# Element-wise work of the mLSTM heads moved from GpSimd to VectorE in a one-layer hybrid trunk

## The chip, the core and the metric

The kernel runs on one core of a Trainium2 chip. The metric is the device time of one launch in microseconds (us); lower is better. The engines named below are PE (TensorE, matmuls), DVE (VectorE), ACT (ScalarE), POOL (GpSimd) and SP (SyncE, which issues every DMA of this kernel). In the code they are `T`, `V`, `A`, `G` and `nc.sync`.

## What is computed

One layer of a hybrid decoder on a prompt of 1024 tokens and on 32 sample tokens (8 sequences of 4). Shapes: width 1024, four mLSTM heads of 128, 512 S5 channels.

```python
proj = rmsnorm(h) @ w_in                       # x_m, z_m, o_m, gates, x_s, z_s
xc = silu(conv4(x_m));  q, k, v = per head of xc, xc, x_m
# chunkwise mLSTM, per head and chunk, m_t the running max:
s   = (q k^T) * exp(b_t - b_s + i_s - m_t)     # causal
num = s v + decay * (q C);  qn = s.sum + decay * (q n)
hA  = num / max(|qn|, exp(-m_t));  C, n = dl * (C, n) + sum wl k (v, 1)
hA  = (layernorm(hA * sigmoid(o)) * ln_head + skip * xc) * silu(z_m)
yB  = gelu(s5_scan(x_s));  yB = yB * sigmoid(yB @ w_glu + b) * silu(z_s)
h   = h + concat(hA, yB) @ w_out
h   = h + sigmoid(h @ w_ple_gate) * rmsnorm(p @ w_ple);  y = rmsnorm(h)
```

The outputs are y and the new states (C, n, m, convolution, S5) of the prompt and of the samples. All of it is fp32.

## The kernel before

Large products are made as three passes, since each fp32 operand is split into a rounded `hi` part and a rest `lo = x - hi` (`mm3`, L123 to L125: hi*hi, hi*lo, lo*hi). In time the program goes through the projections of x_s and o (to about 100 us), the S5 scan (to 240), the mLSTM heads (240 to 400), the rest of the gated unit of S5, called glu here (to about 430), w_out (431 to 540) and w_ple_gate (540 to the end).

The order of PE is written by hand (`tc.manual_schedule`): `turns` runs the generators of two prompt heads (0 and 1, then 2 and 3) in turn, a piece of a sample head between them, and after each piece `take(n)` puts n columns of other matmuls (projections of x_m, z_m, z_s, then the glu) as fill. The order of the other engines, SP too, is made by a scheduler from a simulated timeline, so an instruction that changes its engine shifts others. Each engine works strictly in its order.

What the change touches, for one head and one half of 512 tokens (`mlstm`):

- L1132 loads `nmb` (a row of decay exponents, broadcast by DMA from DRAM); L1133 adds the causal mask `cmask`. L1154 (ACT) takes its exponential and L1155 (DVE) multiplies it with the scores `sps` in PSUM.
- L1137 makes `qps`, L1138 (ACT) copies it to `qp`; L1163 makes `qd = qp * dcb`, which the matmul L1171 reads. L1145 makes `xw` from the transposed `xc`.
- L1175 to L1180 update state and output; `lnorm` (L1206 to L1226) normalises, with a power on POOL at L56; its last four instructions L1226 write what PE transposes at L1188 (`tph`).
- The tail of a half: ACT `sk` L1190, DVE L1191, then L1194 multiplies `sk` with the gate `zt` and a DMA writes it to DRAM.

For the samples (`sample_head`), four times per head: L1298 spreads v over sequence pairs under a mask (`svm`, 96x258), the matmul L1300 makes `sups`, two instructions L1302 add it to the state. L1326 and L1328 (`sample_end`) apply skip and gate of the 32 tokens. `wload` loads the weights of w_out and w_ple_gate; its rest L1353 (`wol`, `wgl`) is made by POOL for odd k and by DVE for even k. In the glu, L1034 makes the rest `yl` of its input, which L124 of `mm3` multiplies; L1482 makes the rest `mlo` of the heads' output.

PSUM pools: `pv` has two buffers (vps, qps, tpxc, sps), `pg` one (all of the sample head), `pt` one (tph).

Of the kernel before, what the change touches and what calls it, by code (L numbers as in the profile page):

```python
# [8 lines left out]
F32 = mybir.dt.float32  # L9
# [3 lines left out]
MUL, ADD, SUB, MAX, MIN = ALU.mult, ALU.add, ALU.subtract, ALU.max, ALU.min  # L13
# [16 lines left out]
def tile_hymba(ctx: ExitStack, tc: tile.TileContext, d: dict, o: list):  # L30
    nc = tc.nc
    (y_p, y_s, o_pC, o_pn, o_pm, o_pconv, o_pre, o_pim, o_sC, o_sn, o_sm, o_sconv, o_sre, o_sim) = o
    V, A, G, T = nc.vector, nc.scalar, nc.gpsimd, nc.tensor
# [307 lines left out]
    skp = hcols[:, 4:8]  # L341
# [85 lines left out]
    k = 1  # L427
# [14 lines left out]
    for tr_, ti_, l0, n in ((rAr, rAi, 3, 3), (rBr, rBi, 6, 4)):  # L442
        for s in range(n):
            k = 1 << s
# [91 lines left out]
    zt = s5p.tile([128, 512], F32, name="zt")  # L536
# [198 lines left out]
    cmask = mlc.tile([128, 128], F32, name="cmask")  # L735
# [341 lines left out]
    mt8 = mo.tile([128, 8, 32], F32, name="mt8")  # L1077
    xcs = mlc.tile([128, 4, 32], F32, name="xcs")
# [42 lines left out]
    def mlstm(h, v1, xc):  # L1121

        Cst = None
        tail = None
        for t in range(2):
            sl = slice(512 * t, 512 * t + 512)
            gc = 8 * h + 4 * t

            nmb = mo.tile([128, 4, 128], F32, tag="nmb", name="nmb", bufs=2)
            dcb = mo.tile([128, 4, 128], F32, tag="dcb", name="dcb", bufs=2)  # L1130
            for t_, x in ((nmb, 0), (dcb, 1)):
                dma(t_, d_row[x, h, 4 * t:4 * t + 4].unsqueeze(0).to_broadcast([128, 4, 128]))  # L1132
            G.tensor_tensor(nmb, nmb, cmask.unsqueeze(1).to_broadcast([128, 4, 128]), op=ADD)  # L1133

            qp = mo.tile([128, 512], F32, tag="qp", name="qp", bufs=2)
            ps = pv([128, 512], "qps")
            T.matmul(ps, Gm[:, h, :], xc[:, sl], start=True, stop=True)  # L1137
            A.copy(qp, ps)  # L1138
            yield
            xw = mo.tile([128, 4, 128], F32, tag="xw", name="xw", bufs=2)  # L1140
            tp = pv([128, 4, 128], "tpxc")
            for c in range(4):
                cc = 4 * t + c
                T.transpose(tp[:, c, :], xc[:, 128 * cc:128 * cc + 128], ident)
            V.tensor_tensor(xw, tp, colv[:, 1, gc:gc + 4].unsqueeze(2).to_broadcast([128, 4, 128]), op=MUL)  # L1145
            yield
            sp = pv([128, 4, 128], "sps")
            for c in range(4):
                cc = 4 * t + c
                T.matmul(sp[:, c, :], xc[:, 128 * cc:128 * cc + 128], qp[:, 128 * c:128 * c + 128],  # L1150
                         start=True, stop=True)
            sd = nmb
            for c in range(4):
                A.activation(sd[:, c, :], nmb[:, c, :], AF.Exp, bias=colv[:, 0, gc + c:gc + c + 1])  # L1154
            V.tensor_tensor(sd, sd, sp, op=MUL)  # L1155
            so4 = mo.tile([128, 4, 128], F32, tag="so4", name="so4", bufs=2)
            dma(so4, d_so[4 * t:4 * t + 4, :, 128 * h:128 * h + 128].rearrange("c p v -> p c v"))
            yield
            if tail is not None:
                tail()  # L1160
                yield
            qd = ml.tile([128, 4, 128], F32, tag="qd", name="qd", bufs=2)
            G.tensor_tensor(qd, qp.rearrange("p (c x) -> p c x", x=128), dcb, op=MUL)  # L1163

            hs = qd
            qn = ml.tile([128, 4], F32, tag="qn", name="qn", bufs=2)
            for c in range(4):
                nu = pn([128, 2, 129], "nu")
                T.matmul(nu[:, 0, :], sd[:, c, :], v1[:, 4 * t + c, :], start=True, stop=Cst is None)
                if Cst is not None:  # L1170
                    T.matmul(nu[:, 0, :], qd[:, c, :], Cst, start=False, stop=True)  # L1171
                T.matmul(nu[:, 1, :], xw[:, c, :], v1[:, 4 * t + c, :], start=True, stop=True)
                Cn = ml.tile([128, 129], F32, tag="Cst", name="Cst", bufs=4)
                if Cst is None:
                    V.tensor_copy(Cn, nu[:, 1, :])  # L1175
                else:
                    V.scalar_tensor_tensor(Cn, Cst, dcb[:, c, 127:128], nu[:, 1, :], op0=MUL, op1=ADD)
                Cst = Cn
                V.tensor_copy(qn[:, c:c + 1], nu[:, 0, 128:129])
                V.scalar_tensor_tensor(hs[:, c, :], so4[:, c, :], 1.0, nu[:, 0, 0:128], op0=ADD, op1=MUL)  # L1180
                if c == 3:
                    lnorm(hs, qn, colv[:, 2, gc:gc + 4], 128, 4)
                yield

            def tail(t=t, sl=sl, hs=hs):
                tp = pt([128, 4, 128], "tph")
                for c in range(4):
                    T.transpose(tp[:, c, :], hs[:, c, :], ident)  # L1188
                sk = ml.tile([128, 512], F32, tag="sk", name="sk", bufs=2)
                A.mul(sk, xc[:, sl], skp[:, h:h + 1])  # L1190
                V.scalar_tensor_tensor(sk, tp.rearrange("p c x -> p (c x)"), lnh[:, h:h + 1], sk, op0=MUL, op1=ADD)  # L1191
                zt = mo.tile([128, 512], F32, tag="zt", name="zt", bufs=2)
                dma(zt, d_z[h, :, sl])
                G.tensor_tensor(sk, sk, zt, op=MUL)  # L1194
                dma(d_m0[t][h], sk)


        fps = pn([128, 129], "fps")
        T.matmul(fps, wk[:, h, :], Cst, start=True, stop=True)
        fo = ml.tile([128, 129], F32, tag="Cst", name="fo", bufs=4)  # L1200
        A.mul(fo, fps, SC)
        dma(o_pC[0, 0, h], fo[:, 0:128])
        V.tensor_copy(pnc[:, h:h + 1], fo[:, 128:129])
        yield
        tail()
        yield  # L1206

# [28 lines left out]
    def sample_head(h):  # L1236
# [13 lines left out]
        for i in range(3):  # L1250
# [7 lines left out]
        v3 = ml.tile([96, 129], F32R, tag="sv3", name="sv3")  # L1258
# [5 lines left out]
                               op0=MUL, op1=SUB)  # L1264
# [30 lines left out]
        for b0, nb in ((0, 2), (2, 2), (4, 2), (6, 2)):  # L1295
            ups = pg([128, 2, 129], "sups")
            vm = ml.tile([96, 2, 129], F32R, tag="svm", name="svm", bufs=1)
            G.tensor_tensor(vm[:, :nb], v3.bitcast(F32).unsqueeze(1).to_broadcast([96, nb, 129]),  # L1298
                            bmask[:, b0:b0 + nb].unsqueeze(2).to_broadcast([96, nb, 129]), op=MUL)
            T.matmul(ups[:, :nb, :], kw3, vm[:, :nb], start=True, stop=True)  # L1300
            for b in range(nb):
                V.scalar_tensor_tensor(c0[:, b0 + b, :], c0[:, b0 + b, :], dl[:, b0 + b], ups[:, b, :],  # L1302
                                       op0=MUL, op1=ADD)
            if b0 < 6:
                yield
# [4 lines left out]
    def sample_end():  # L1310
        tp = pg([32, 128], "tpn")
        T.transpose(tp, snc.rearrange("p b h -> p (b h)"), ident)
        ob = ml.tile([32, 128], F32, tag="skw", name="sob", bufs=1)
        A.copy(ob, tp)
        dma(o_sn[0].rearrange("b h k -> (b h) k"), ob)

        hs = shs[:, :, 0:128]
        V.scalar_tensor_tensor(hs[:, 0, :], sos, 1.0, hs[:, 0, :], op0=ADD, op1=MUL)
        lnorm(hs, shs[:, 0, 128:129], senm, 128, 1)
        tp = pg([128, 4, 32], "tpsh")  # L1320
        T.transpose(tp.rearrange("p h t -> p (h t)"), hs[:, 0, :], ident)
        zt = ml.tile([128, 4, 32], F32, tag="sxv", name="szt")
        dma(zt, d_z[0:4, :, 1024:1056].rearrange("h p t -> p h t"))
        sk = ml.tile([128, 4, 32], F32, tag="sqm", name="ssk")
        for h in range(4):
            G.tensor_scalar(sk[:, h, :], xcs[:, h, :], skp[:, h:h + 1], None, op0=MUL)  # L1326
            V.scalar_tensor_tensor(sk[:, h, :], tp[:, h, :], lnh[:, h:h + 1], sk[:, h, :], op0=MUL, op1=ADD)
        G.tensor_tensor(mt8[:, 0:4, :], sk, zt, op=MUL)  # L1328

    def prompt_end():  # L1330
        tp = pt([4, 128], "tpn")
# [12 lines left out]
    def wload(src, k, q, nm, use=None):  # L1344
        raw = pW.tile([128, 512], F32, tag="Wraw", name="Wraw", bufs=4)
        dma(raw, src[128 * k:128 * k + 128, 512 * q:512 * q + 512])
        pool = pW1 if q else pW
        hi = pool.tile([128, 512], F32R, tag="Whi", name=f"{nm}h{k}", bufs=8)
        lo = pool.tile([128, 512], F32R, tag="Wlo", name=f"{nm}l{k}", bufs=8)
        A.copy(hi, raw)  # L1350
        if use is not None:
            use(raw, k, q)
        (G if k % 2 else V).tensor_tensor(lo, raw, hi.bitcast(F32), op=SUB)  # L1353
        return hi, lo

    KO = (4, 5, 6, 7, 0, 1, 2, 3)
# [175 lines left out]
    for q in range(2):  # L1532
        for k in range(2):
            raw = pW.tile([128, 512], F32, tag="Wraw", name="Wraw", bufs=4)
# [140 lines left out]
```

## Time and profile before

| | |
|---|---|
| median of 3 runs | 663.01 us (662.4 to 669.05) |
| the profiled execution's own time | 664.25 us |
| span of the profiled execution | 662.5 us |
| mean granted TensorE clock | 0.982 of 2.4 GHz |
| PE busy | 615.7 us (93%) |
| DVE busy | 451.9 us (68%) |
| ACT busy | 254.8 us (38%) |
| POOL busy | 134.3 us (20%) |

Busy time says how long an engine had an instruction under way, whether it moved data or stood. Shares are over the whole span; stages differ, so the rows further down go stage by stage.

### The profile page before, as it was taken

To read this page: it belongs to the slowest core of one execution; us is meant where nothing else is said; L and a number is where in the kernel's file an instruction comes from. 1 tells how busy PE (TensorE), PEld (TensorE's weight loads), DVE (VectorE), ACT (ScalarE), POOL (GpSimd) and SP (SyncE) were. 2 spreads that over 40 slices of the span, in tenths; PEclk is the share of its full clock that TensorE was granted. 3 is DMA by queue.
4 is the path that set the end of the run, shared out by engine and by line. 5 is a ranking of instruction groups with operands and counts; after the bars stand their busy time and mean duration, and the time that the engine had idled before them with its cause. 6 is when DMAs were issued, how large, how long until landed. Compare 5 with 4: busy or idle time off the path is not lost.

```text
span 662.5 us, 11620 instructions
## 1 busy us (share of the span) xinstructions
PE 615.7 (93%) x4072; PEld 539.0 (81%) x4072; DVE 451.9 (68%) x1345; ACT 254.8 (38%) x622; POOL 134.3 (20%) x149
## 2 busy tenths in 40 slices
PE   5999999999999998987989897799999999999995
PEld 3999998999989986776978796677888776788885
DVE  6788969999998945996757689955222325566435
ACT  5653733333343555342331335444112225533332
POOL 6830200000000003142323523533001113010000
PEclk9999999999999997997999998899999999999999
DMA  8813345356544348362633555576341264412111
GB/s 261 240 57 57 98 145 137 90 150 152 145 109 122 99 104 237 116 209 65 171 114 118 175 165 164 187 241 213 111 152 67 92 235 141 146 49 109 63 64 64
DMA packets 112418, 90.03 MB, mean 136 GB/s; under 512 B 34080, under 2 KB 94900, under 8 KB 112360
## 3 DMA queue, kind: packets, MB, share of 16 engines
q1 hardware_dynamic: 112360, 89.29, 45.4%
q8 instruction: 32, 0.52, 0.3%
q14 instruction: 26, 0.21, 0.1%
HBM read 61.68 MB, written 27.58 MB: 135 GB/s over the span
## 4 chain that ended last, share of the span: by engine, by line
PE 60%; DVE 12%; issue 12%; DMA 11%; ACT 2%; SPq 2%; POOL 1%; POOLq 0%; DVEq 0%; ACTq 0%
PE po L1494 5%; PE po L1495 5%; PE po L1496 4%; PE po L1603 3%; PE po L1604 3%; PE po L1605 3%; PE ps_xs L123 2%; PE ps_o L123 2%; PE ps_xs L124 2%; PE ps_xs L125 2%; PE ps_o L124 2%; PE ps_o L125 2%; DMA xt<-in_x_prompt 2%; SPq L36 2%; PE ps_zs L123 2%
## 5 line engine op out<-in xcount | busy, mean ns | idle before, releaser
L1603 PE MATMUL po<-wgh,hTh 128*128 128x512 f32 (+1 forms) x136 | 52.1, 383 | 0.7 <-ACT g_t L1606 0.7
L1605 PE MATMUL po<-wgh,hTl 128*128 128x512 f32 (+1 forms) x136 | 51.5, 379 | 0.0
L1604 PE MATMUL po<-wgl,hTh 128*128 128x512 f32 (+1 forms) x136 | 51.4, 378 | 0.0
L123 PE MATMUL ps_o<-hi_o,aTh 128*128 128x264 f32 (+2 forms) x136 | 41.0, 301 | 0.0
L123 PE MATMUL ps_zs<-aTh,hi_zs 128*128 128x256 f32 (+2 forms) x96 | 39.9, 416 | 0.0
L125 PE MATMUL ps_o<-hi_o,aTl 128*128 128x264 f32 (+2 forms) x136 | 39.4, 290 | 0.0
L124 PE MATMUL ps_o<-lo_o,aTh 128*128 128x264 f32 (+2 forms) x136 | 39.4, 290 | 0.0
L123 PE MATMUL ps_xm<-aTh,hi_xm 128*128 128x256 f32 (+2 forms) x96 | 35.2, 367 | 0.0
L123 PE MATMUL ps_zm<-aTh,hi_zm 128*128 128x256 f32 (+2 forms) x96 | 32.1, 334 | 1.3 <-ACT zc L721 1.3
L1494 PE MATMUL po<-woh,mh 128*128 128x512 f32 x80 | 32.7, 409 | 0.0
L1495 PE MATMUL po<-wol,mh 128*128 128x512 f32 x80 | 32.0, 400 | 0.0
L123 PE MATMUL ps_xs<-aTh,hi_xs 128*128 128x256 f32 (+2 forms) x96 | 31.3, 326 | 0.4 <-ACT xs L287 0.4
L125 PE MATMUL ps_zs<-aTh,lo_zs 128*128 128x256 f32 (+2 forms) x96 | 31.6, 329 | 0.0
L124 PE MATMUL ps_zs<-aTl,hi_zs 128*128 128x256 f32 (+2 forms) x96 | 31.6, 329 | 0.0
L1496 PE MATMUL po<-woh,mlo 128*128 128x512 f32 x80 | 31.5, 394 | 0.0
L1503 DVE TENSOR_TENSOR hTl<-tr,hTh 128x512 fp32r<-128x512 f32 x16 | 11.0, 690 | 29.8 <-ACT hTh L1502 29.8
L125 PE MATMUL ps_xm<-aTh,lo_xm 128*128 128x256 f32 (+2 forms) x96 | 31.4, 327 | 0.0
L124 PE MATMUL ps_xm<-aTl,hi_xm 128*128 128x256 f32 (+2 forms) x96 | 31.4, 327 | 0.0
L125 PE MATMUL ps_xs<-aTh,lo_xs 128*128 128x256 f32 (+2 forms) x96 | 31.3, 326 | 0.0
L124 PE MATMUL ps_xs<-aTl,hi_xs 128*128 128x256 f32 (+2 forms) x96 | 31.3, 326 | 0.0
L125 PE MATMUL ps_zm<-aTh,lo_zm 128*128 128x256 f32 (+2 forms) x96 | 31.0, 323 | 0.0
L124 PE MATMUL ps_zm<-aTl,hi_zm 128*128 128x256 f32 (+2 forms) x96 | 31.0, 323 | 0.0
(594 smaller groups left out, 1916.4 us busy)
## 6 DMA issues: line engine op xcount, KB each, us to landing
xt<-in_x_prompt SPq DMA_DIRECT2D x15, 512.0 KB
Wraw<-in_w_out SPq DMA_DIRECT2D x16, 256.0 KB
Wraw<-in_w_ple_gate SPq DMA_DIRECT2D x16, 256.0 KB
d_h<-xt SPq DMA_DIRECT2D x8, 512.0 KB
h_t<-d_h SPq DMA_DIRECT2D x8, 512.0 KB
out<-g_t SPq DMA_DIRECT2D x14, 256.0 KB
mt<-d_m SPq DMA_DIRECT2D x10, 256.0 KB
d_us<-xs SPq DMA_DIRECT2D x32, 72.0 KB
```

The source lines that it names most:

```text
L36: nc.sync.dma_start(out, in_)
L123: T.matmul(ps, wh, xh, start=first, stop=False)
L124: T.matmul(ps, wh, xl, start=False, stop=False)
L125: last_mm[0] = T.matmul(ps, wl, xh, start=False, stop=last).ins
L1494: T.matmul(ps, mh[:, k % 4, :], hi, start=k == 4, stop=False)
L1495: T.matmul(ps, mh[:, k % 4, :], lo, start=False, stop=False)
L1496: T.matmul(ps, mlo[:, k % 4, :], hi, start=False, stop=k == 3)
L1503: V.tensor_tensor(hTl[i][:, 4 * q:4 * q + 4, :], tp, hi.bitcast(F32), op=SUB)
L1603: T.matmul(ps[:, :b - a], hTh[i][:, k, :], hi[:, ws], start=k == 4, stop=False)
L1604: T.matmul(ps[:, :b - a], hTh[i][:, k, :], lo[:, ws], start=False, stop=False)
L1605: T.matmul(ps[:, :b - a], hTl[i][:, k, :], hi[:, ws], start=False, stop=k == 3)
```

## The change

Every element-wise instruction that the heads, the sample heads and `wload` gave to POOL is given to DVE, with the same operands: per head and half L1133, L1163 and L1194 (8 of each), L1298 (16), L1326 (4), L1328 (1), and the 16 of L1353 with odd k. POOL keeps the powers (L56 and others), L1482 and some work of earlier stages. Nothing else is edited.

```diff
-            G.tensor_tensor(nmb, nmb, cmask.unsqueeze(1).to_broadcast([128, 4, 128]), op=ADD)
+            V.tensor_tensor(nmb, nmb, cmask.unsqueeze(1).to_broadcast([128, 4, 128]), op=ADD)
...
-            G.tensor_tensor(qd, qp.rearrange("p (c x) -> p c x", x=128), dcb, op=MUL)
+            V.tensor_tensor(qd, qp.rearrange("p (c x) -> p c x", x=128), dcb, op=MUL)
...
-                G.tensor_tensor(sk, sk, zt, op=MUL)
+                V.tensor_tensor(sk, sk, zt, op=MUL)
...
-            G.tensor_tensor(vm[:, :nb], v3.bitcast(F32).unsqueeze(1).to_broadcast([96, nb, 129]),
+            V.tensor_tensor(vm[:, :nb], v3.bitcast(F32).unsqueeze(1).to_broadcast([96, nb, 129]),
...
-            G.tensor_scalar(sk[:, h, :], xcs[:, h, :], skp[:, h:h + 1], None, op0=MUL)
+            V.tensor_scalar(sk[:, h, :], xcs[:, h, :], skp[:, h:h + 1], None, op0=MUL)
...
-        G.tensor_tensor(mt8[:, 0:4, :], sk, zt, op=MUL)
+        V.tensor_tensor(mt8[:, 0:4, :], sk, zt, op=MUL)
...
-        (G if k % 2 else V).tensor_tensor(lo, raw, hi.bitcast(F32), op=SUB)
+        V.tensor_tensor(lo, raw, hi.bitcast(F32), op=SUB)
```

The scheduler puts the moved instructions among those of DVE. Three places follow; a row that begins with + stands there in the changed kernel, with - in the one before, without a sign in both.

DVE, heads 0 and 1, second half (about 282 to 286 us before): the first `nmb` in the queue.

```order
 L1212 TENSOR_TENSOR ln_3881<-ln_3881,colv 128x4
-L1177 SCALAR_TENSOR_TENSOR Cst<-Cst,dcb,nu 128x129
-L1179 COPY qn<-nu 128x1
-L1219 BN_AGGR bmv<-bst 128x2
+L1133 TENSOR_TENSOR nmb<-nmb,cmask 128x512
+L1219 BN_AGGR bmv<-bst 128x2
+L1213 RECIPROCAL ln_3881<-ln_3881 128x4
+L1090 SCALAR_TENSOR_TENSOR xc<-xm,hcols,xc 128x1024
+L1177 SCALAR_TENSOR_TENSOR Cst<-Cst,dcb,nu 128x129
+L1179 COPY qn<-nu 128x1
 L1180 SCALAR_TENSOR_TENSOR qd<-so_3728,nu 128x128
```

The addition L1133, and behind it a convolution step L1090 of the next head, now stand ahead of the state update L1177.

DVE, heads 0 and 1, end of the first half's `lnorm` (about 299 to 303 us before).

```order
 L1191 SCALAR_TENSOR_TENSOR sk<-tph,hcols,sk 128x512
+L1163 TENSOR_TENSOR qd<-qp,dcb 128x512
+L1298 TENSOR_TENSOR svm<-sv_4091,bmask 96x258
 L1224 SCALAR_TENSOR_TENSOR ln_3924<-bmv,ln_3922 128x4
+L1194 TENSOR_TENSOR sk<-sk,zt 128x512
 L1226 TENSOR_SCALAR qd<-qd,ln_3922,ln_3924 128x128 x4
 L1191 SCALAR_TENSOR_TENSOR sk<-tph,hcols,sk 128x512
+L1163 TENSOR_TENSOR qd<-qp,dcb 128x512
+L1194 TENSOR_TENSOR sk<-sk,zt 128x512
 L1270 TENSOR_TENSOR ssd<-smb,ssps 32x32
```

Three instructions come to stand ahead of the four L1226 of head 1, and two behind them.

DVE, glu (about 407 to 411 us before).

```order
+L1034 SCALAR_TENSOR_TENSOR yl<-yb,yh 128x256 x2
+L1224 SCALAR_TENSOR_TENSOR ln_5253<-bmv,ln_5251 128x4
+L1226 TENSOR_SCALAR qd<-qd,ln_5212,ln_5214 128x128 x4
 L1050 SCALAR_TENSOR_TENSOR tg<-tg,yb 128x256
 L1050 SCALAR_TENSOR_TENSOR tg<-tg,ysb 128x32
-L1034 SCALAR_TENSOR_TENSOR yl<-yb,yh 128x256
-L1213 RECIPROCAL ln_5682<-ln_5682 128x1
-L1034 SCALAR_TENSOR_TENSOR yl<-yb,yh 128x256
 L1052 TENSOR_TENSOR zg<-tg,zg 128x256
```

The first two `yl` now stand ahead of the four L1226 of head 2, where before they stood behind them.

## Rows read from the trace of the kernel before

**Rows 1.** Part 1 of the page: busy us, share, instructions by engine.

```profile
PE 615.7 (93%) x4072; PEld 539.0 (81%) x4072; DVE 451.9 (68%) x1345; ACT 254.8 (38%) x622; POOL 134.3 (20%) x149
```

**Rows 2.** Windows: us, PE, PEld, DVE, ACT, POOL busy, granted clock, DMA share, GB/s.

```profile
240.00:260.00 20.00, 15.48 (x82) 12.56 (x82) 6.18 (x25) 9.83 (x25) 4.07 (x4) 0.84 0.81 211
260.00:280.00 20.00, 18.49 (x139) 16.38 (x139) 19.21 (x59) 8.50 (x18) 2.59 (x3) 0.99 0.33 101
280.00:300.00 20.00, 15.80 (x100) 13.26 (x99) 18.76 (x64) 7.94 (x21) 8.57 (x8) 1.00 0.64 198
400.00:420.00 20.00, 15.07 (x98) 13.70 (x98) 19.72 (x53) 11.50 (x25) 11.59 (x8) 0.91 0.51 155
440.00:460.00 20.00, 20.00 (x146) 15.47 (x145) 11.47 (x15) 10.66 (x18) 6.98 (x5) 1.00 0.76 238
304.00:308.00 4.00, 4.00 (x16) 3.84 (x16) 1.26 (x6) 0.77 (x2) 1.48 (x2) 0.50 0.43 140
424.00:428.00 4.00, 4.00 (x30) 3.56 (x28) 3.56 (x10) 1.96 (x3) 1.38 (x1) 0.57 0.40 136
```

**Rows 3.** Timeline of PE: start, duration, instruction, idle before and its releaser.

```profile
254.11 2.07 PE L1137 MATMUL qps<-xc,Gm 128*128 128x512 f32 x2 [2.97 <-ACT v L1105]
...
279.81 0.36 PE L1300 MATMUL sups<-svm,skw 96*128 96x258 f32 x1 [1.41 <-DVE sc L1302]
...
301.73 1.15 PE L1188 MATMUL tph<-ident,qd 128*128 128x128 f32 x4 [4.14 <-DVE qd L1226]
...
370.31 0.94 PE L1150 MATMUL sps<-qp,xc 128*128 128x128 f32 x6 [1.75 <-DVE xw L1145]
...
408.96 0.38 PE L124 MATMUL ps_g<-yl,hi_g 128*128 128x256 f32 x1 [1.94 <-DVE yl L1034]
...
421.89 0.38 PE L124 MATMUL ps_g<-yl,hi_g 128*128 128x256 f32 x1 [2.74 <-DVE yl L1034]
```

**Rows 4.** Groups of POOL: busy us, mean ns, idle before.

```profile
L1194 POOL TENSOR_TENSOR sk<-sk,zt 128x512 f32<-128x512 f32 x8 | 11.9, 1494 | 7.8 <-DVE ln L1221 7.7
L1133 POOL TENSOR_TENSOR nmb<-nmb,cmask 128x512 f32<-128x512 f32 x8 | 11.3, 1407 | 66.6 <-DMA nmb<-d_row 64.2 <-DVE sv L1260 1.9 <-DVE sv L1259 0.6
L1353 POOL TENSOR_TENSOR wol<-Wraw,woh 128x512 fp32r<-128x512 f32 x8 | 11.0, 1369 | 24.5 <-ACT woh L1350 24.4
...
L1298 POOL TENSOR_TENSOR svm<-sv,bmask 96x258 fp32r<-96x258 f32 x16 | 10.3, 645 | 63.5 <-PE sups L1300 42.0 <-DVE sv L1265 16.0 <-DMA raw_g<-in_w_glu 5.6
L1163 POOL TENSOR_TENSOR qd<-qp,dcb 128x512 f32<-128x512 f32 x8 | 10.2, 1275 | 13.5 <-DMA d_z<-ztmp 5.8 <-ACT qp L1138 3.3 <-PE tph L1188 2.8
```

**Rows 5.** Groups of DVE: busy us, mean ns, idle before.

```profile
L1052 DVE TENSOR_TENSOR zg<-tg,zg 128x256 f32<-128x256 f32 x16 | 9.8, 622 | 0.0
L1302 DVE SCALAR_TENSOR_TENSOR sc<-sc,sdc,sups 128x129 f32<-128x129 f32 x32 | 9.7, 339 | 0.6 <-PE sups L1300 0.5
L1353 DVE TENSOR_TENSOR wol<-Wraw,woh 128x512 fp32r<-128x512 f32 x8 | 7.5, 933 | 4.6 <-ACT woh L1350 4.6
L1034 DVE SCALAR_TENSOR_TENSOR yl<-yb,yh 128x256 fp32r<-128x256 f32 x16 | 7.4, 480 | 5.6 <-ACT yh L1033 5.5
```

**Rows 6.** Timeline of DVE: single instructions, start and duration.

```profile
295.54 1.10 DVE L1226 TENSOR_SCALAR qd<-qd,ln,ln 128x128 f32<-128x128 f32 x4
...
300.26 2.08 DVE L1226 TENSOR_SCALAR qd<-qd,ln,ln 128x128 f32<-128x128 f32 x4
...
398.93 0.69 DVE L1353 TENSOR_TENSOR wol<-Wraw,woh 128x512 fp32r<-128x512 f32 x1 [0.48 <-ACT woh L1350]
...
420.36 1.81 DVE L1034 SCALAR_TENSOR_TENSOR yl<-yb,yh 128x256 fp32r<-128x256 f32 x2
```

**Rows 7.** Timeline of POOL: single instructions, with what they waited for.

```profile
284.36 1.28 POOL L1133 TENSOR_TENSOR nmb<-nmb,cmask 128x512 f32<-128x512 f32 x1 [0.59 <-DVE sv L1259]
...
300.24 1.26 POOL L1194 TENSOR_TENSOR sk<-sk,zt 128x512 f32<-128x512 f32 x1
...
420.16 1.40 POOL L1482 TENSOR_TENSOR mlo<-mt,mh 128x512 fp32r<-128x512 f32 x1
```

## The prediction, made before the changed kernel had run

> **What bounds the kernel now.** I began with the busy times by engine [rows 1]: PE works 615.7 of 662.5 us, so there are some 47 us of PE idling to win at most, and whatever is won must be read where PE stands. DVE, with 451.9 us, looks half free, but that is a mean. The windows [rows 2] show stages: from 260 to 300 us DVE is busy 19.21 and 18.76 of every 20 us, from 400 to 420 it is busy 19.72, and in just these stretches PE loses time (1.5, 4.2 and 4.9 us per window). From 440 us on PE is busy 20.00 of 20 and stays so nearly to the end. So a matmul that starts earlier before 430 us ends the kernel earlier by the same amount, and an element-wise instruction after 440 us costs or gives nothing while it stays in time for PE.
>
> The timeline of PE then names the waits [rows 3]. Between 240 and 430 us the largest are: 2.97 us at 254.11 for ACT's copy `v` (it stands on ACT behind the exponentials of `nmb`), 1.41 us at 279.81 for the state update of the sample head, 4.14 us at 301.73 for the last `qd` of `lnorm`, 1.75 us at 370.31 for `xw`, and 1.94 and 2.74 us at 408.96 and 421.89 for `yl` of the glu. Only the first hangs on a moved instruction by its data; the others wait for DVE.
>
> Two more costs sit in these stages. First the clock: after 301.73, PE is busy 4.00 of 4 us with a granted clock of 0.50, the lower of its two levels (1.2 GHz), and after 421.89 it is 4.00 of 4 at 0.57 [rows 2]. Each stretch follows an idle time of PE [rows 3]. The 20 us from 240 have a mean clock of 0.84 and those from 400 of 0.91: at full clock they would give back about 0.16 x 20 = 3.2 and 0.09 x 20 = 1.8 us, and the one after 421.89 (1 - 0.57) x 4 = 1.7 us.
>
> Second, DVE stands while POOL works: four L1226 take 1.10 us alone and 2.08 us beside an L1194 of POOL [rows 6, 7]; the eight L1353 of DVE average 933 ns though one alone takes 0.69 [rows 5, 6]. Going through all such pairs I count about 18 us of extra DVE time, some 13 of them beside instructions that the change moves. The Trainium skill ("SBUF — State Buffer", Who interferes with whom) says that DVE and GpSimd share a port pair as an exclusive lock, and that a DVE instruction with two SBUF inputs, or in a two-port mode, blocks fully until the other's instruction ends. The rows above agree with it. By the same section the moved instructions, most of which read two operands from SBUF, can themselves be held up on DVE by the powers and by L1482, which stay on POOL. What stays can hold DVE up now as well: two `yl` took 1.81 us beside an L1482 [rows 6, 7], against twice some 0.4.
>
> **The change part by part.** On POOL the moved instructions cost 1.3 to 1.5 us each, 0.65 for `svm` [rows 4]. On DVE, 40 of 128x512 cost what one L1353 alone costs, 0.69 [rows 6], less some overlap of neighbours, say 0.65: 26 us. The 16 `svm` (96x258) lie between L1302's 0.34 and L1052's 0.62; I take 0.42, nearest to `yl` of 256 columns, whose mean 0.48 still holds stalls [rows 5]: 7 us (5.4 to 9.9). The five of the samples' end are at most 1.5. DVE gains 34 us of work and loses about 13 us of stalls: 452 becomes some 472 us. What that does goes by stage.
>
> *246 to 262 us.* `nmb` waits for its DMA either way. After that the addition takes 0.65 instead of 1.3, ahead of exponentials and `v`. ACT's order also puts the first `v` ahead. I take -0.5 (0 to -2 if the slow clock that follows shortens).
>
> *262 to 303 us.* Here DVE is full, so all that is added counts: five `svm` 2.1, two `nmb` 1.2, one `qd` and one `sk` 1.3 stand ahead of the last four L1226, sum 4.6 us. The stalls that go are four (0.6 and 1.0 in two convolution steps and an L55 beside `nmb`, 1.0 beside `qd`, 1.0 beside `sk` [rows 6, 7]), sum 3.6. And `nmb` now waits on DVE for a DMA: POOL began it at 284.36 [rows 7], while its new place in DVE's order comes at about 283; behind it are queued the convolution, the state update L1177 and `lnorm`, for which PE waits. That costs 0.8 (0 to 1.5). DVE has only 0.8 and 1.2 us of idle time per window there [rows 2] to absorb it. Sum +1.5, from -1 to +4: `tph` at 303 instead of 301.73.
>
> *303 to 345 us.* DVE has room there. `svm` is no longer queued behind `nmb` on POOL, but L1302, and the DMA of the finished state behind it, comes a little later: +0.5 (-1 to +1).
>
> *345 to 400 us.* `xw`, for which PE waited 1.75 us [rows 3], stood behind four L1226 and a power held up on POOL behind `nmb`. Without that `nmb` on POOL the chain is about 1.8 us shorter, and the changed order puts both `xw` ahead of the L1226: -1.7 (0 to -2). Two `nmb` wait for their DMA here as well, in front of `lnorm` and of L1302; there is idle time of DVE for it.
>
> *400 to 431 us.* DVE is full, and stalls beside POOL are some 6 us, about 4 of them beside L1353 and L1194. Added are two L1353 and two L1194, 2.6 us, for stalls of 4 that go; and the order puts the first two `yl` ahead of four L1226 (1.1 us). So the first wait for `yl` goes from 1.94 to about 0.5. At the second (2.74), the stall is beside L1482, which stays; I take 1.7 off it for the work ahead of it that is done sooner, and its slow clock, worth 1.7, I count half gone, like the one after the first. Sum -1.4 - 1.7 - 1.4 = -4.5 (0 to -8).
>
> *431 us to the end.* The remaining `wol` and all `wgl` move from 1.37 us on POOL to 0.69 on DVE, in a stretch where DVE is busy 11.47 of 20 [rows 2] and PE is full: 0. The cover is PE's own queue of matmuls on weights that are already there; without it an L1353 would cost 0.69 each on the way to PE.
>
> The sum is -0.5 + 1.5 + 0.5 - 1.7 - 4.5 = -4.7 us. Against the profiled execution's 664.25 this is 659.5; the median of the runs, 663.01, lies 1.2 below that execution, so the forecast is **658.3 us**.
>
> **Rivals.** *The glu and the clock give all back* (faster). The stalls' end lets DVE run ahead by 3 us or more at 400 us; both waits for `yl` fall below 0.3 us and both slow stretches go. To the sum come another 0.6 + 1.0 + 2.0, and 1.5 if the one at 304 shortens too: 653. For it: DVE's stalls in that stage outweigh its additions; against it: L1482 and the powers remain on POOL.
>
> *DVE's queue stands before the DMA* (slower). All of the four `nmb` of second halves now block everything behind them, state updates, `lnorm`, `svm` and `sups`. If their rows land 1.5 us or more after DVE reaches them, 262 to 303 us costs +5 instead of +1.5, the heads 2 and 3 lose 2 instead of winning 1.7, and DVE reaches the glu late, so that the 4.5 there are not won: -0.5 + 5 + 0.5 + 2 = +7 on 663.01, 670 us. It decides when PE's wait at the last `tph` of that stage goes above 7 us. For it: DVE is busy 19 of 20 us there, so that nothing absorbs a wait. Against it: other instructions are ahead of `nmb` in the queue, and only one of the four is seen to be late by my count.
>
> *Nothing moves* (no change). What the stalls give back the added 34 us of work take; the wait for `xw` goes and that for `tph` grows by as much, the glu keeps its waits since L1482 stalls the same `yl`: 663.
>
> *Every stall comes back* (faster). If each of the 13 us of stalls beside moved instructions lay on PE's path and the added work did not, the time would be 663 - 13 = 650 us. Against it: DVE gates PE only in the windows named above. This is what the section of the Trainium skill named above gives if it is read alone.
>
> **How the numbers follow.** About 1%, 6.6 us, can be told from no change: faster is below 656.4, slower above 669.6. I give the forecast 0.36, with a spread of its own from 655 to 662; the rival with glu and clock 0.26; every stall 0.04; no change 0.20; the slower one 0.14, some two thirds of it beyond 669.6. Faster: 0.26 + 0.04 + a fourth of 0.36 = 0.39. Slower: 0.09. Within 1%: 0.52. The range from 651 to 667 takes in the faster rival with glu and clock, the forecast's bounds and no change; it leaves out the every-stall case and the slower rival, a little under 2 in 10.
>
> **What would show it.** Right: the four L1226 before `tph` at 1.1 us; `tph` at about 303 us with an idle time of 4 to 6 us before it; no wait of PE for `xw`; waits for `yl` below 1 us; DVE busy near 472 and POOL near 66 us; PE as full as before from 431 us. Wrong: an idle time of DVE of over 1.5 us before an `nmb`, released by a DMA; powers on POOL that take much longer than before; slow clock over more than 20 us in all; new PE waits for weights after 431 us.

## The result: 1% faster, and the profile after

The changed kernel took 659.19 us (median of 10 runs, 657.25 to 661.8), the kernel before 666.23 us (10 runs, 662.4 to 672.24). The ratio is 0.9896, 95% interval [0.9861, 0.9931]: 6.9 us faster, 4.6 to 9.3. The forecast was 658.3 us and a gain of 4.7 us; the two profiled executions differ by 5.0 us (664.25 and 659.28).

Part 1 of the page after, to be held against [rows 1]:

```profile
PE 613.3 (93%) x4072; PEld 536.2 (82%) x4072; DVE 464.8 (71%) x1406; ACT 254.7 (39%) x622; POOL 69.3 (11%) x88
```

POOL has lost 65 us (69.3 left, 66 forecast), DVE has 13 us more (472 in all were forecast, 464.8 it is). The moved instructions last 35 us there in all, while the durations of all of DVE's instructions together rose by 19 us (from 528 to 547), so some 16 us of stalls went, where the prediction counted 13. The groups of DVE now (busy us, mean ns, idle before):

```profile
L1353 DVE TENSOR_TENSOR wol<-Wraw,woh 128x512 fp32r<-128x512 f32 x16 | 10.7, 689 | 9.1 <-ACT woh L1350 9.1
L1298 DVE TENSOR_TENSOR svm<-sv,bmask 96x258 fp32r<-96x258 f32 x16 | 6.7, 417 | 0.0
L1133 DVE TENSOR_TENSOR nmb<-nmb,cmask 128x512 f32<-128x512 f32 x8 | 5.5, 686 | 7.5 <-DMA nmb<-d_row 7.5
```

L1353 is back at 689 ns where it averaged 933 [rows 5], and `svm` costs 0.417 us where 0.42 was taken. DVE stood 7.5 us for the DMA of `nmb`, 3.6 of it in the first two, at 250.67 and 253.50, where it has room.

The windows after (columns as in [rows 2]); the three short ones hold all the slow clock there is between 240 us and the start of w_out:

```profile
240.00:260.00 20.00, 14.97 (x89) 12.91 (x88) 7.18 (x29) 9.65 (x26) 0.00 (x0) 0.91 0.80 216
260.00:280.00 20.00, 17.55 (x133) 15.34 (x132) 18.59 (x59) 8.48 (x18) 0.00 (x0) 1.00 0.31 95
280.00:300.00 20.00, 16.39 (x100) 13.40 (x100) 17.91 (x69) 7.84 (x21) 2.46 (x2) 1.00 0.66 199
400.00:420.00 20.00, 14.21 (x99) 12.11 (x98) 20.00 (x60) 10.86 (x23) 8.16 (x5) 1.00 0.54 165
...
253.00:261.00 8.00, 4.86 (x19) 3.79 (x20) 4.28 (x15) 4.02 (x14) 0.00 (x0) 0.79 1.07 349
299.00:309.00 10.00, 6.89 (x33) 5.78 (x33) 7.55 (x24) 1.44 (x2) 0.00 (x0) 0.66 0.33 105
418.00:425.00 7.00, 6.58 (x39) 5.88 (x40) 6.55 (x18) 3.42 (x7) 1.38 (x1) 0.76 0.76 237
```

The same short windows of the kernel before, around its four slow stretches:

```profile
252.00:262.00 10.00, 7.89 (x25) 5.44 (x26) 4.89 (x11) 7.07 (x21) 4.09 (x4) 0.66 1.02 335
299.00:309.00 10.00, 7.27 (x30) 6.36 (x30) 5.57 (x17) 1.44 (x2) 4.39 (x4) 0.66 0.33 105
409.00:415.00 6.00, 5.76 (x33) 5.55 (x34) 6.00 (x20) 1.49 (x3) 1.41 (x1) 0.72 0.32 104
423.00:429.00 6.00, 5.49 (x39) 4.90 (x39) 5.53 (x14) 2.44 (x4) 1.38 (x1) 0.72 0.53 177
```

Reading them: the clock is 1.0 or half of that, so (1 - clock) x length x 2 is the time at the lower level. Before it is 6.8 + 6.8 + 3.4 + 3.4 = 20.4 us, after 3.4 + 6.8 + 3.4 = 13.6 us. The stretch at 410 us is gone and the first is halved.

Timeline of PE after (columns as in [rows 3]):

```profile
302.77 1.15 PE L1188 MATMUL tph<-ident,qd 128*128 128x128 f32 x4 [3.11 <-DVE qd L1226]
...
368.55 1.13 PE L1150 MATMUL sps<-qp,xc 128*128 128x128 f32 x8
...
408.58 0.38 PE L124 MATMUL ps_g<-yl,hi_g 128*128 128x256 f32 x1 [1.54 <-DVE yl L1034]
...
417.94 0.38 PE L123 MATMUL ps_g<-yh,hi_g 128*128 128x256 f32 x1 [2.10 <-ACT tg L1048]
```

`tph` is 1.0 us later than before, the wait for `xw` (1.75 us) is gone, the first wait for `yl` fell only from 1.94 to 1.54, and in place of the 2.74 us for `yl` stands one of 2.10 for `tg`, which comes from ACT.

### The profile page after: what moved, and what is told of

It reads as the page before. It is cut to its first block, busy times and chain, and to the rows that moved or that the text cites. A ratio compares the mean times of both kernels' runs of the same rounds, so it can differ in the third digit from the quotient of the medians.

```text
span 657.5 us, 11568 instructions
## 1 busy us (share of the span) xinstructions
PE 613.3 (93%) x4072; PEld 536.2 (82%) x4072; DVE 464.8 (71%) x1406; ACT 254.7 (39%) x622; POOL 69.3 (11%) x88
## 4 chain that ended last, share of the span: by engine, by line
PE 60%; DVE 16%; DMA 14%; SPq 4%; issue 3%; ACT 2%; POOL 0%; POOLq 0%; DVEq 0%; ACTq 0%
PE po L1494 5%; PE po L1495 5%; PE po L1496 5%; PE po L1603 4%; PE po L1605 4%; PE po L1604 4%; SPq L36 4%; DMA nmb<-d_row 2%; PE ps_xs L123 2%; PE ps_o L123 2%; PE ps_xs L124 2%; PE ps_xs L125 2%; PE ps_o L125 2%; PE ps_o L124 2%; DMA xt<-in_x_prompt 2%
## 5 line engine op out<-in xcount | busy, mean ns | idle before, releaser
L56 POOL TENSOR_TENSOR ln<-ln,mhalf 128x4 f32<-128x4 f32 (+1 forms) x9 | 11.8, 1319 | 197.8 <-DVE ln L55 130.9
L1494 PE MATMUL po<-woh,mh 128*128 128x512 f32 x80 | 32.6, 407 | 0.0
```

Source lines behind the costliest of these rows:

```text
L56: G.tensor_tensor(out, tmp, mhalf[:p, :n], op=ALU.pow)
L1494: T.matmul(ps, mh[:, k % 4, :], hi, start=k == 4, stop=False)
```

## Experiments

Each kernel was timed in five rounds against the kernel before. Ratios are to it, with 95% intervals, and the gains are worked out from them. By the medians the gains differ from these by up to 1.3 us: 8.0 for the heads alone, 7.0 for the change.

One thing limits all of them: the scheduler makes its order anew for each kernel. By the traces 15 to 110 of DVE's unmoved instructions come in another order than in the kernel that the edit was made to (27 of 1345 with L1133 alone moved), and some of ACT and SP too; only the change without L1353 of w_ple_gate keeps nearly all of it. In the others a difference is that of the engine and of the order together.

| kernel | ratio | interval | us of gain |
|---|---|---|---|
| the change | 0.9896 | 0.9861 to 0.9931 | 6.9 |
| heads alone (L1133, L1163, L1194) | 0.9861 | 0.9826 to 0.9896 | 9.2 |
| L1133 alone | 0.9917 | 0.9884 to 0.9950 | 5.5 |
| L1163 and L1194 alone | 0.9903 | 0.9870 to 0.9935 | 6.5 |
| svm alone | 1.0001 | 0.9977 to 1.0026 | 0.0 |
| L1353 alone | 0.9951 | 0.9920 to 0.9983 | 3.3 |
| heads and L1353 of w_out | 0.9901 | 0.9869 to 0.9933 | 6.6 |
| change without L1133 | 0.9985 | 0.9964 to 1.0006 | 1.0 |
| change without svm | 0.9886 | 0.9857 to 0.9916 | 7.6 |
| change without L1353 of w_ple_gate | 0.9900 | 0.9864 to 0.9937 | 6.7 |
| change, L1482 on VectorE too | 0.9961 | 0.9934 to 0.9988 | 2.6 |
| change, with idle work on GpSimd | 1.0050 | 1.0026 to 1.0074 | -3.3 |
| before, L1133 left out | 0.9945 | 0.9919 to 0.9971 | 3.7 |

**One group on VectorE, the rest as before.** The edit is always the engine's letter of the lines named:

```diff
-            G.tensor_tensor(nmb, nmb, cmask...
+            V.tensor_tensor(nmb, nmb, cmask...
```

> Of the kernel before, only the head instructions L1133, L1163 and L1194 go to VectorE; svm, the samples' end and all of L1353 stay on GpSimd. Theory by stages (each stage's wait on PE has its own cause): the wait of PE for xw near 370 us goes (-1.7), the first slow-clock stretch near 254 us shortens (-0.8 or so), the glu wins about half of its 2.3, nothing changes at the start of w_ple_gate near 548 us: 3 us faster than before (1 to 5). Rival, it is the weights' rests L1353 beside which VectorE stood: within 1 us of before.

9.2 us faster. The rival falls (the weights are not needed), but the size was three times mine. In its profile no wait for `xw` is left, `tph` is 0.8 us earlier than before instead of 0.9 later as in the change (all such shifts are counted from the first `vps` matmul, the first of the heads, at 239 us), and the time from the second `tph` at 376 us to w_out is 3.1 us shorter, where half of 2.3 was expected.

> Of the kernel before, only svm (L1298) goes to VectorE. Theory by stages: VectorE is full from 260 to 303 us and still stands beside GpSimd there, five svm of 0.42 add to it, so tph of that stage is 1 to 2 us later; the wait near 323 us stays about 1 us. In all 0 to 2 us slower than before. Rival, GpSimd's own queue (svm behind nmb) was the cost of the sample head: the wait near 323 us goes, 1 us faster.

No change in time, as the theory allowed. In its profile `tph` is 3.7 us later, more than the 1 to 2 expected; and no wait of 0.35 us or more is left near 323 us, as the rival said, but that did not pay.

> Of the kernel before, only the rests L1353 of w_out and w_ple_gate with odd k go to VectorE. Theory by stages: nothing changes up to 395 us, the glu wins 1 to 1.5, the start of w_ple_gate near 548 us wins 1.4: 2.5 us faster than before (1 to 4). Rival, L1353 carries the whole: 5 us or more faster.

3.3 us faster, within the theory's 1 to 4; but its profile does not show the parts. Against the profile before, the time from 376 us to w_out is 0.6 us shorter (1 to 1.5 was expected), and from w_out to the end nothing is won (0.1 us lost).

> Of the kernel before, only L1133 (the mask added to nmb) goes to VectorE. With it the heads' group was 9.2 us faster than before, and the changed kernel without it only 1.0. Theory, nmb on GpSimd is what held the heads up (its 1.3 us stand between a DMA and the exponentials, qp and the powers queue behind it, VectorE stands beside it): 5 to 8 us faster than before, with no wait of PE for xw near 370 us. Rival, it is only the sum of small stalls: the three head instructions share the 9.2, nmb alone gives 3 or less.

5.5 us faster, within the theory's 5 to 8, and the wait for `xw` is gone. The next kernel shows the same stage with L1133 still on POOL:

> Of the kernel before, only L1163 and L1194 go to VectorE. Theory of nmb: nothing of the wait for xw near 370 us goes, only the stalls beside these two (4 us of VectorE time) against 10 us of added work; 0 to 2.5 us faster than before. Rival, the stalls beside L1226 ahead of tph carry the gain: 4 us or more faster.

6.5 us faster: the rival was right on the size, though the wait for `xw` is still there, as the theory said. The rows, first L1133 on VectorE, then L1163 and L1194 on VectorE:

```profile
368.30 1.05 PE L1150 MATMUL sps<-qp,xc 128*128 128x128 f32 x8
```

```profile
368.00 1.16 PE L1150 MATMUL sps<-qp,xc 128*128 128x128 f32 x8 [1.80 <-DVE xw L1145]
```

So the wait goes when L1133 moves to VectorE, and not when L1163 and L1194 move. That holds for every kernel timed: none of the eight with L1133 on VectorE has a wait of 0.9 us or more for `xw` or `qp` near 370 us, and each of the other six has one of 1.6 to 2.4 us. That the addition on POOL is its cause is not shown by this, since one of the six has no addition at all, the kernel with L1133 left out (its line numbers are one less: L1153 is L1154, L1137 is L1138). Its rows of ACT and PE:

```profile
364.73 1.28 ACT L1153 ACTIVATE nmb<-nmb,colv 128x128 f32<-128x128 f32 x4 [1.67 <-DMA nmb<-d_row]
365.91 1.04 ACT L1137 COPY qp<-qps 128x512 f32<-128x512 f32 x2
```

```profile
366.52 0.66 PE L1143 MATMUL tpxc<-ident,xc 128*128 128x128 f32 x4 [1.96 <-ACT qp L1137]
```

There PE waits for `qp`, which stands on ACT behind the exponentials of both heads; with L1133 on VectorE the trace has it between them. So the order counts as well as the engine.

The two parts give 5.5 and 6.5 us, together 9.2: they do not add up.

> The heads' group on VectorE, and the odd rests of w_out as well; svm and the odd rests of w_ple_gate stay on GpSimd. Heads alone were 9.2 us faster than before, all weights alone 3.3, both with the samples' end 7.6. Theory, in the glu VectorE is full, and what the heads' group has won there the rests of w_out take back: 7 to 8.5 us faster than before, 1 to 2 slower than the heads alone. Rival, the gains add up and the samples' end costs: 10 us or more faster than before.

6.6 us faster, 2.6 less than the heads alone (the intervals overlap, and by the medians it is 0.9): nothing adds up here, the rival falls. That the glu takes it back is not shown by this.

**One group back on GpSimd.**

> The changed kernel with L1133 (the mask added to nmb) back on GpSimd. Theory by stages: the gain near 370 us is nmb's, since the power of lnorm stood behind it on GpSimd, so the wait for xw there is back in part (+1 to +1.7); against that VectorE waits no more for nmb's DMA near 283 us (1.49 us in the changed kernel) and has two additions less, so tph near 303 us is up to 2 us earlier. In all within 1.5 us of the changed kernel. Rival, queueing behind the DMA is what the change loses: 2 us or more faster than the changed kernel.

1.0 us faster than before, which its interval does not tell apart from zero, so 5.9 of the 6.9 us are lost; both theories were wrong. Its profile shows something that I had left out. Timelines of POOL, DVE, ACT and PE:

```profile
288.09 2.50 POOL L1133 TENSOR_TENSOR nmb<-nmb,cmask 128x512 f32<-128x512 f32 x1 [2.38 <-DMA nmb<-d_row]
```

```profile
288.16 1.27 DVE L1090 SCALAR_TENSOR_TENSOR xc<-xm,hcols,xc 128x1024 f32<-128x1024 f32 x1
289.36 1.25 DVE L1221 TENSOR_TENSOR ln<-ln,bmv 128x4 f32<-128x4 f32 x1
```

```profile
290.62 0.69 ACT L1154 ACTIVATE nmb<-nmb,colv 128x128 f32<-128x128 f32 x2 [2.87 <-POOL nmb L1133]
291.23 0.56 ACT L1138 COPY qp<-qps 128x512 f32<-128x512 f32 x1
```

```profile
291.84 0.66 PE L1144 MATMUL tpxc<-ident,xc 128*128 128x128 f32 x4 [1.60 <-ACT qp L1138]
```

POOL's addition took 2.50 us, about twice its usual time, beside a DVE instruction with two operands (L1090), which took its usual 1.27 us; the small L1221 behind it then took 1.25 instead of 0.15 us, until POOL was done. So POOL is held up beside DVE as well as DVE beside POOL. The exponentials wait for it, `qp` stands behind them on ACT, and PE waits 1.60 us for `qp` there, a wait that the change does not have. `tph` of head 1 is 1.5 us later than in the change. Near 370 us PE again stands, 1.63 us, for `qp` and not for `xw`. Against the profile of the change, the stretches from 264 to 302 and from 344 to 374 us are 2.9 and 2.1 us longer; which share of the 5.9 us comes from these two waits is not shown.

> The changed kernel with svm (L1298) back on GpSimd, which then does little else but powers. Theory by stages: VectorE loses five svm of 0.42 in the full stretch from 260 to 303 us, but svm takes 0.61 instead of 0.42 on the path to sups, and it makes VectorE stand again where it meets two-operand instructions: tph near 303 us 0.5 to 1.5 us earlier, in all 0 to 2 us faster than the changed kernel. Rival, one engine without a hand-over is better for the chain from L1302 over svm to sups: 1 us or more slower.

7.6 us faster than before, 0.7 more than the change, within the theory's 0 to 2 and not told apart from zero by the intervals. `tph` is 1.2 us earlier than before where the change has it 0.9 later. The difference, 2.1 us, is what the prediction charged to the five `svm` in that stretch.

> The changed kernel with the odd rests of w_ple_gate alone back on GpSimd. If the 1.4 us that PE wins near 548 us in the changed kernel come from these rests (a buffer of the raw weights comes free sooner, the next load lands sooner), they are lost again: 1.4 us slower than the changed kernel, with a wait of PE for g_t there. Rival, they come from another order on ScalarE or from chance: as fast as the changed kernel, and no wait there.

As fast as the change: the rival was right. PE's wait near 548 us in the profile before is absent here too. The same matmul, first before, then here:

```profile
549.88 0.50 PE L1603 MATMUL po<-wgh,hTh 128*128 128x512 f32 x1 [0.72 <-ACT g_t L1606]
```

```profile
546.95 0.50 PE L1603 MATMUL po<-wgh,hTh 128*128 128x512 f32 x1
```

From the first w_out matmul (L1494) to the first `pe` matmul (L1582, w_ple, at 553 us before) PE wins 1.2 us here, as in the change. The other profiles with these rests on POOL range from 1.4 won (`svm` alone moved) to 1.2 lost (heads and L1353 of w_out). So the rests of w_ple_gate do not cause it; one profiled execution of before may simply have been late there.

**The port.**

```diff
             V.tensor_tensor(qd, qp.rearrange("p (c x) -> p c x", x=128), dcb, op=MUL)
+            G.tensor_tensor(qp, qp, dcb.rearrange("p c x -> p (c x)"), op=MUL)
```

and likewise behind L1194 and behind the odd L1353 of w_out.

> The changed kernel, with 24 additional instructions on GpSimd whose results nobody reads: after each L1163 and L1194 and after each odd rest of w_out on VectorE, GpSimd makes the same product or difference once more, into an operand that is no longer needed. VectorE's work is that of the changed kernel. Theory, port: VectorE stands beside these 1.3 us instructions as it did before, 5 to 8 us of extra VectorE time, and loses half of the change's gain: 2 to 4 us slower than the changed kernel. Rival, the gain came from shorter instructions and from the new order, not from freeing the port: within 1 us of the changed kernel.

10.2 us slower than the change and 3.3 slower than before: the theory's direction, three times its size; the rival in its form (within 1 us) falls. DVE does the same work, but is busy 475.4 us instead of 464.8, 10.6 us more. Around 420 us, DVE and then POOL (this kernel's L1486 is L1482, its L1196 one of the additions), and last the same three `yl` of DVE in the change:

```profile
419.69 4.32 DVE L1034 SCALAR_TENSOR_TENSOR yl<-yb,yh 128x256 fp32r<-128x256 f32 x3
```

```profile
419.23 1.68 POOL L1486 TENSOR_TENSOR mlo<-mt,mh 128x512 fp32r<-128x512 f32 x1
420.87 1.45 POOL L1196 TENSOR_TENSOR zt<-sk,zt 128x512 f32<-128x512 f32 x1
422.40 1.33 POOL L1486 TENSOR_TENSOR mlo<-mt,mh 128x512 fp32r<-128x512 f32 x1
```

```profile
417.49 2.17 DVE L1034 SCALAR_TENSOR_TENSOR yl<-yb,yh 128x256 fp32r<-128x256 f32 x3
```

Three `yl` took 4.32 us, about 1.4 us each, as long as one POOL instruction; in the change the same three took 2.17. This kernel also holds buffers a little longer, some 33 of DVE's 1406 instructions come in another order than in the change, and the clock was lower (0.9776 over its 12 runs against 0.9877), so not all of the 10.2 us need be the port.

**L1482 too.**

```diff
-                G.tensor_tensor(mlo, mt, mh.bitcast(F32), op=SUB)
+                V.tensor_tensor(mlo, mt, mh.bitcast(F32), op=SUB)
```

> The changed kernel with L1482 (the rest mlo of the heads' output) on VectorE as well. Theory, port: VectorE still stands 1.6 us beside L1482 in the glu of the changed kernel (L1052 1.18 and L1034 1.49); it gains these and gets two of 0.69, so yl of the last pass comes up to 0.5 us earlier: 0 to 1 us faster than the changed kernel. Rival, ScalarE's queue: the last large wait of the glu is for tg, behind yh that waits for its load, and VectorE's time does not matter there: no change within 0.5 us.

4.3 us slower than the change: both theories were wrong. The glu itself won (the first w_out matmul is 4.6 us earlier than before, in the change 3.6), but then PE stood:

```profile
435.93 0.43 PE L1361 MATMUL po<-Wraw,mt 128*32 128x128 f32 x8 [1.79 <-DMA Wraw<-in_w_out]
```

The scheduler had put the loads of these weights, on SP, behind the store of `zg`. The order of SP, + for this kernel and - for the change:

```
-L36 DMA Wraw<-in_w_out 128x512 x3
 L36 DMA h_5822<-in_x_sample 32x1024
-L36 DMA Wraw<-in_w_out 128x512
 L36 DMA xt_5914<-in_x_prompt 128x1024
 L36 DMA d_m_73<-zg 128x4x256
 L36 DMA Wraw<-in_w_out 128x512 x4
```

The store waits for DVE's last `zg`, so the four loads were issued from 431.71 us instead of 425.89. The wait accounts for 1.8 of the 4.3 us; the rest is open.

**L1133 left out.** The line is deleted from the kernel before.

> The kernel before with L1133 left out altogether (the causal mask is not added, so the scores of later tokens are not cut off); no engine does it. Theory, VectorE carries the eight additions nearly free (their 5.5 us lie in waits for the same DMA): 0 to 2 us faster than nmb on VectorE alone. Rival, VectorE pays for them in the full stretch from 260 to 303 us: 3 us or more faster than nmb on VectorE alone.

3.7 us faster than before, not more than with L1133 on VectorE (5.5, the intervals overlap). So the rival falls: what VectorE pays for the additions is not seen in the time. It is not shown to be nothing, since this kernel has its own order, with the wait of 1.96 us for `qp` shown above that the kernel with L1133 on VectorE does not have.

## Why the prediction came out, point by point

The sum was right, and some of its terms were wrong by as much as 2 us in both directions; that they cancelled is luck. So is part of the 658.3 against 659.19: the three runs of the kernel before that the forecast started from had a median 3.2 us below that of the ten (663.01 and 666.23), and the gain was 2.2 us larger than forecast. The shift of PE in the two profiles, counted from the first `vps` matmul at 239 us:

| stretch (us before) | predicted | measured |
|---|---|---|
| to 264 | -0.5 | -0.9 |
| 264 to 302 (`tph` of head 1) | +1.5 | +1.9 |
| to 344 (next `tph`) | +0.5 | -1.3 |
| to 376 | -1.7 | -0.9 |
| to 431 (w_out) | -4.5 | -2.3 |
| to 553 (first `pe`) | 0 | -1.2 |
| to the end | 0 | -0.3 |
| sum | -4.7 | -5.1 |

*To 264 us*: the size was near, the reason was not. The shorter addition was to end PE's waits for `v` sooner; PE's idle time there rose from 4.5 to 5.0 us, with this wait after (the 2.97 us of before are in [rows 3]):

```profile
256.14 2.07 PE L1137 MATMUL qps<-xc,Gm 128*128 128x512 f32 x2 [3.49 <-ACT v L1105]
```

What was won is the halved slow clock (3.4 us less of it), which the prediction had in its range but not in its -0.5.

*To 302 us*: right, and by the mechanism named. DVE waited 1.49 us for the DMA of `nmb` in front of the state update (0.8 was taken, the bound given was 1.5), the L1226 took 1.11 us instead of 2.08, and `tph` came at 302.77 (303 was forecast). The parts as written add up to +1.8 (4.6 - 3.6 + 0.8), not to the +1.5 taken:

```profile
284.60 0.69 DVE L1133 TENSOR_TENSOR nmb<-nmb,cmask 128x512 f32<-128x512 f32 x1 [1.49 <-DMA nmb<-d_row]
...
302.29 1.11 DVE L1226 TENSOR_SCALAR qd<-qd,ln,ln 128x128 f32<-128x128 f32 x4
```

*To 344 us*: wrong. PE's clock is slow from 300.4 to 307.2 us in the change and from 301.2 to 308.1 before. Since `tph` is later, 2.4 us of the slow time fall into PE's waiting, before only 0.5; at half speed, half of the difference, 0.9 us, is won back. PE's idle time there also fell, by 0.4 us, so the cost of 0.5 us that was forecast does not show. A wait that takes up slow clock costs less than it shows.

*To 376 us*: the wait for `xw` went as forecast (-1.6 up to the first `tph` at 374 us). The cause named, the power and the L1226 held up behind `nmb` on POOL, is in part argued: L1133 on VectorE takes the wait away, but leaving L1133 out leaves one of 1.96 us for `qp`. 0.6 us came back at the second `tph`, where PE waits for DVE's `sk` 1.41 us instead of 0.77.

*The glu*: half of the term, and the step that was most wrong. It assumed that the first `yl` would come about 1.5 us sooner. DVE was full (20.00 of 20), and the wait fell by 0.4 us. The second wait changed its cause: `tg` stands on ACT behind a `yh` that waits for its load, rows of ACT after:

```profile
417.11 0.42 ACT L1033 ACTIVATE yh<-yb 128x256 fp32r<-128x256 f32 x1 [1.80 <-DMA yb<-d_y]
417.44 0.46 ACT L1048 ACTIVATE tg<-ps_g,hcols 128x256 f32<-128x256 f32 x1
```

The stretch of slow clock at 410 us went, as half counted.

*The end*: 0 was forecast; the 1.2 us up to 553 us came without the moved instructions there, as the kernel with L1353 of w_ple_gate on POOL showed.

*The clock* had more of the whole than I gave it. In each of the 14 profiles (before, the change, 12 experiments), the time from 239 us to w_out less PE's idle time and less half the slow time is 153 to 157 us. For the change, idle time fell from 27.2 to 25.9 us and slow time from 20.4 to 13.6: of these two the clock is the larger (3.4 against 1.3 us). The two make 4.7 us where 3.6 were won, so the split is rough. Over the runs, the mean clock is 0.9795 before (76 runs, mean 665.8 us) and 0.9877 after (10 runs, 659.3 us). Among the runs of before, 0.01 of clock goes with 3.9 us; by that an estimated 3.2 of the 6.5 us between these means go with the clock. Which way this works is not shown: slow stretches start in or behind waits of PE, so fewer waits can be the cause of the higher clock. The heads alone have a clock of 0.9830 and 657.4 us (6 runs): 1.4 us by the same slope, so by this estimate their gain is mostly in waits.

The rival *DVE's queue stands before the DMA* had its wait (7.5 us in all, 1.49 at the one place), but not its price. Two of the signs named for being wrong were met without harm: an idle time of DVE of over 1.5 us in front of `nmb` (1.59 and 2.05 us, at 250.67 and 253.50), and one power on POOL of 2.36 us at 402.04, where before none of the heads' took over 1.5. Of the signs for being right, PE's idle time before `tph` was 3.11 us (4 to 6 was given), and the waits for `yl` did not fall below 1 us. *Every stall comes back* did not happen either: some 16 us of stalls went, and the time fell by 6.9. The kernel with idle work on POOL shows that work on POOL beside DVE can cost 10 us, the order being another there too. The Trainium skill ("SBUF — State Buffer", Who interferes with whom) says that whoever issues first holds the pair for the whole instruction and the other blocks, so that POOL can be the one held up. The row of L1133 above, 2.50 us on POOL beside DVE's L1090, agrees in that POOL was the one held up; since its start is recorded 0.07 us before that of L1090, it does not show who issued first.

Two readings of the rows were too narrow. PE loses time not "in just these stretches" where DVE is full: from 240 to 260 us it lost 4.5 us with DVE busy 6.18 of 20 [rows 2]. And the list of the largest waits leaves out 1.55 us at 246.1 (for `v`), 1.54 at 290.5, 1.62 at 337.8 (for `qp`) and 1.47 at 400.3 (for `tg`), all longer than the 1.41 that it has; three of these four wait for ACT.

What stays open: what of the gains is the freed port and what is the new order, since the kernels differ in both; and why the gains of the parts do not add up. It fits that each removes slow stretches that the next cannot remove again, but L1133 alone won 5.5 us at nearly the clock of before (0.9812), so this is not shown.

The heads alone are the fastest version that ran (0.9861). Against the change the intervals overlap, each up to the other's ratio, and the medians are 1.3 us apart (657.88 and 659.19); that they are better is likely, not shown.

## What to carry to other kernels

Work that two engines share through a port is judged where the slower one hands over: here GpSimd's 1.3 us additions stood between a DMA, ScalarE's queue and PE, and moving them alone won 5.5 us though a busy VectorE got 5.5 us more to do. Try first what others wait for, and leave where it is what has slack: the `svm` and the weights' rests brought nothing beyond the heads. Where a scheduler makes the order, moving an instruction moves others too: read the new order of every queue before putting a gain down to the engine. A reordered DMA queue can take back a gain, as the loads of w_out did when L1482 was moved.

## What the runs showed that was not expected

- In stretches that no edit touches, single executions differ: the first `vps` matmul starts between 236.3 and 240.1 us in the 14 profiles, in part since five of them have a wait of 1.3 to 2.3 us near 219 us and nine have none. Stage shifts below 1 us from single profiles mean little; they were counted from behind this point for that reason.
- The clock's slow time from 239 us to w_out ranged from 10.2 to 30.7 us in these profiles. The 30.7 belong to the slowest run of the kernel with L1133 alone, at a mean clock of 0.973.
